# Feature-major projections: one 512-column matmul for the high weights, and the two halves summed by VectorE

## The chip, the cores and the metric

One core of a Trainium2 chip runs the whole program. The metric is the device time of one execution in microseconds (us). The engines are TensorE (PE, matmuls; PEld, its weight loads), VectorE (DVE), ScalarE (ACT), GpSimd (POOL) and SyncE (SP, which here only issues transfers).

## The reference

Four layers, each of another kind, act one after the other on x of 256 tokens by 2048 features, all in fp32. After each, `h = layer_norm(ALPHA * h + out)`.

```python
def ssd_mixer(h, w_in, ...):        # 8 groups, 64 heads of 64, state 128, chunks of 128 tokens
    z, xbc, dt = split(h @ w_in)
    xbc = silu(causal_depthwise_conv(xbc, conv_w, conv_b))       # 4 taps; 6144 features
    ... # scan over chunks, gate with silu(z), rms norm by group
    return y @ w_out
def fox_mixer(h, w_in, f_bias, w_out):   # 16 heads of 128
    q, k, v, z, f = split(h @ w_in)
    o = causal_block_attention(q, k, v, scale, cumsum(log_sigmoid(f + f_bias)))
    return (o * silu(z)) @ w_out
def mla_mixer(...):                      # 16 heads, latent q and kv, rope
    ...
    return (o * silu(z)) @ w_out
def s5_mixer(...):                       # 128 groups of 16 features, complex state of 64
    u, z = split(h @ w_in)
    ... # y = scan(u) + d * u
    y = gelu(y)
    y = y * sigmoid(y @ w_glu + b_glu) * silu(z)
    return y @ w_out
```

What matters here are the large products `h @ w` with 2048 inputs: the change touches those whose result is needed with features on the partitions.

## The kernel before

Every fp32 operand of a large product is split into a high part (rounded to the matmul's fp32r type) and a low part (the rest), and a product is the sum of three matmuls: high by high, high by low, low by high (`mm3`, L105 to L109). Weights come from memory in halves of 512 KB: SP's queue loads a half into one of seven `raw` buffers, ACT rounds it to `whi` (L100), DVE subtracts to get `wlo` (L101); there are four buffers of each. Activations hT (`hh`, `hl`) lie in SBUF with features on partitions, as 16 blocks (kb) of 128 features by 256 tokens.

A token-major projection (`proj_tok`, tile `pt`) holds activations still and moves 512 weight columns. A feature-major one (`proj_T`, L126 to L128, with its steps from L117) holds a 128x128 weight block still and moves the 256 tokens; per kb three matmuls of 256 columns add into one PSUM tile, and 16 kb make a projection. It runs 144 times with 128 weight columns: 48 in ssd (`conv`, tile `cps`), 48 in fox (q, k and z of 16 heads; `fox_q`, `fox_k`, `zps`), 16 in mla (`zps`), 16 for s5's z (`zps`) and 16 for its glu (`gps`); and twice with fewer, for ssd's dt (64, `dps`) and fox's f (16, `fps`). Readers take the result out of PSUM: `conv` by an ACT scale (L466) and three DVE multiply-adds (L468) for the taps, fox q and k by an ACT copy, the z gates by an ACT tanh and a DVE product.

Around it, in ssd: `decays` makes the running sums `acsT` (L487) from dt; POOL loads and broadcasts rows of them into `arena` (L504, L506); DVE turns these into decays (L510, L535); POOL multiplies and adds on `xs` (L557, L562, L587); after its last step in a group (the gate, L562) a normalization follows, and its result is transposed by PE into `ypt` (L605). In s5, a scan on DVE (L1165 to L1171) runs beside the z projections; then come the `near` and `far` matmuls (L1311, L1320) and transfers of `shifts` on POOL's queue (L1146).

The program is written in one order, in which `tick` (once per weight half) and `defer(n, ...)` (run n ticks later) interleave stages. A tile scheduler then orders each engine's instructions by its own cost model.

Of the kernel before, what the change touches and what calls it, by code (L numbers as in the profile page):

```python
# [11 lines left out]
F32 = mybir.dt.float32  # L12
# [18 lines left out]
class Core:  # L31
# [57 lines left out]
    def half(self, src, i, n=2048, spare=None):  # L89

        nc = self.nc
        if self.loads:
            self.loads.pop(0)()
        r = self.raw([P, n // 2], "raw")
        nc.sync.dma_start(r, src[:, i * (n // 2):(i + 1) * (n // 2)])
        if spare:
            hi, lo = (pool.tile([P, n // 2], F32R, tag=t, bufs=b, name=f"w_{t}") for pool, t, b in spare)
        else:
            hi, lo = (self.wp.tile([P, n // 2], F32R, tag=t, bufs=4, name=t) for t in ("whi", "wlo"))
        nc.scalar.copy(hi, r)  # L100
        nc.vector.tensor_tensor(lo, r, hi, op=ALU.subtract)  # L101
        return hi, lo
# [14 lines left out]
    def proj_T_steps(self, src, hT, ps, m=P, order=range(KB)):  # L117

        for i in range(2):
# [12 lines left out]
    def proj_tok(self, srcs, aT, n=512, before=None, tail=None, spare=None):  # L132
# [10 lines left out]
        while h < N:  # L143
# [26 lines left out]
    def proj_Tk(self, srcs, aT):  # L170
# [4 lines left out]
        for q, src in enumerate(srcs):  # L175
            for i in range(2):
                w = self.half(src, i)
                for j in range(2):
                    kb = 4 * q + 2 * i + j
                    a = [x[kb] for x in aT]  # L180
# [86 lines left out]
    def out_layer(self, li, parts, gb_tiles, spare, out=None):  # L267
# [10 lines left out]
        hT = ([None] * KB, [None] * KB)  # L278
# [38 lines left out]
        def turn(t, k0, nk):  # L317
            c = k0 // 4
            if t == 0 and k0 % 4 == 0:
                for i, n in enumerate("hl"):  # L320
                    x = self.hp.tile([P, 4, T], F32R, tag=f"h{n}{c}", name=f"h{n}{c}")
                    hT[i][4 * c:4 * c + 4] = [x[:, k] for k in range(4)]
                    tiles[i].append(x)
# [4 lines left out]
            hi, lo = (x[c][:, k0 % 4:k0 % 4 + nk, t * P:(t + 1) * P] for x in tiles)  # L328
# [3 lines left out]
        tiles = ([], [])  # L332
# [91 lines left out]
def ssd(C, hT, out):  # L424
# [3 lines left out]
    with C.tc.tile_pool(name="ssd", bufs=1) as sp, C.tc.tile_pool(name="ssd_c", bufs=1) as vp, C.tc.tile_pool(name="ssd_t", bufs=1) as tp:  # L428
# [45 lines left out]
        def decays():  # L474
            dps = C.acc("dps")
            C.proj_T(A["ssd_dt"], hT, dps[0:NH, 0:T], m=NH)
            x = arena[0:NH, 0:T]
            nc.vector.tensor_scalar(x, dps[0:NH, 0:T], dtb, None, op0=ALU.add)
# [137 lines left out]
        for g in range(G):  # L616
# [3 lines left out]
                           [[(C.hp, f"h{n}{c}", 1) for n in "hl"] for c in range(4)], out)  # L620


def fox(C, hT, out):
# [3 lines left out]
    with pool(name="fox", bufs=1) as fp, pool(name="fox_t", bufs=2) as tp, \  # L627
# [13 lines left out]
        fps = C.acc("fps")  # L641
        C.proj_T(A["fox_f"], hT, fps[0:H, 0:T], m=H)
        x, lf, one = V[2][0:H, 0, 0:T], V[2][0:H, 0, T:], V[2][0:H, 1, 0:T]
        nc.vector.tensor_scalar(x, fps[0:H, 0:T], fb, None, op0=ALU.add)
# [33 lines left out]
        def head(h):  # L678
# [36 lines left out]
            C.defer(1, C.attend(logits, lambda: V[h // 4], h % 4, finish, shift=cq[:, h, :]))  # L715
            zps = C.acc("zps")
            C.proj_T(A["fox_z"][h], hT, zps[:, 0:T])
            th = tp.tile([P, T], F32, tag="th", name="th")
            nc.scalar.activation(th, zps[:, 0:T], AF.Tanh, scale=0.5)
            nc.vector.scalar_tensor_tensor(th, th, 1.0, zps[:, 0:T], op0=ALU.add, op1=ALU.mult)  # L720
# [4 lines left out]
        for _ in steps:  # L725
# [3 lines left out]
                           [[(C.hp, f"h{n}{c}", 1) for n in "hl"] for c in range(4)], out)  # L729
# [20 lines left out]
def mla(C, hT, out):  # L750
# [3 lines left out]
    with C.tc.tile_pool(name="mla", bufs=1) as mp, C.tc.tile_pool(name="mla_w", bufs=1) as wp, C.tc.tile_pool(name="mla_t", bufs=2) as tp:  # L754
# [84 lines left out]
        for h in range(H):  # L839
            zps = C.acc("zps")  # L840
            C.proj_T(A["mla_z"][h], hT, zps[:, 0:T])
            th = tp.tile([P, T], F32, tag="th", name="th")
            nc.scalar.activation(th, zps[:, 0:T], AF.Tanh, scale=0.5)
            nc.vector.scalar_tensor_tensor(zs[h], th, 1.0, zps[:, 0:T], op0=ALU.add, op1=ALU.mult)
# [267 lines left out]
def s5(C, hT, out):  # L1112
# [8 lines left out]
    with C.tc.tile_pool(name="s5", bufs=1) as sp, C.tc.tile_pool(name="s5_w", bufs=1) as wp, C.tc.tile_pool(name="s5_t", bufs=1) as tp:  # L1121
# [11 lines left out]
        uX, U = {}, {}  # L1133
# [49 lines left out]
        def u_strip(ft):  # L1183
            x = uX[ft] = sp.tile([P, L, 4, NC], F32, tag=f"ux{ft}", name=f"ux{ft}")
# [42 lines left out]
        def turn2(ft, ut, w):  # L1227
            un = U[ft] = (wp if ft == 3 else sp).tile([P, 4, 4, NC], F32, tag=f"un{ft}", name=f"un{ft}")
# [54 lines left out]
        def z_tile(kb):  # L1283
            zps = C.acc("zps")
            C.proj_T(A["s5_z"][kb], hT, zps[:, 0:T])
            th = tp.tile([P, T], F32, tag="th", name="th", bufs=3)
            nc.scalar.activation(th, zps[:, 0:T], AF.Tanh, scale=0.5)
            nc.vector.scalar_tensor_tensor(zs[kb], th, 1.0, zps[:, 0:T], op0=ALU.add, op1=ALU.mult)

        yh, yl = [None] * KB, [None] * KB  # L1290
# [64 lines left out]
        def gelu(ft, yf):  # L1355
            h4 = sp.tile([P, 4, T], F32R, tag=f"ux{ft}", name=f"yh4{ft}")
            l4 = (wp if ft == 3 else sp).tile([P, 4, T], F32R, tag=f"un{ft}", name=f"yl4{ft}", bufs=1)
            for gq in range(4):
                kb = 4 * gq + ft
                yh[kb], yl[kb] = h4[:, gq], l4[:, gq]  # L1360
# [14 lines left out]
        for kb in range(KB):  # L1375
            gps = C.acc("gps")
            C.proj_T(A["s5_glu"][kb], (yh, yl), gps[:, 0:T], order=order)
            s = tp.tile([P, T], F32, tag="th", name="sg", bufs=3)
            nc.scalar.activation(s, gps[:, 0:T], AF.Tanh, bias=bg[:, kb:kb + 1], scale=0.5)
# [8 lines left out]
                           [((sp, f"ux{c}", 1), (wp if c == 3 else sp, f"un{c}", 1)) for c in range(4)], out)  # L1388
# [106 lines left out]
```

## Time and profile before

| | |
|---|---|
| median of 3 runs | 2107.67 us (2106.01 to 2112.61) |
| the profiled execution | 2112.38 us, of which the span is 2110.6 |
| granted TensorE clock in it | 0.982 |
| HBM traffic | 374.32 MB by DMA, mean 177 GB/s |
| matmul instructions | 14409 |

The profile shows one execution. PE's busy time comes from matmuls that overlap, so what one costs is read from the distance between starts; `PEclk` is the clock granted to PE, 1.00 being full speed. A row in brackets, `[7.24 <-issue]`, gives the idle time before an instruction and what ended it; `issue` means that nothing in the profile ended it. In the table of windows each pair is busy time and, in brackets, instructions.

### The profile page before, as it was taken

Reading aid. Unit: us, or ns where it says so; the run is one execution under the profiler, and the core shown is the slowest. Engines: PE = TensorE matmul, PEld = TensorE weight load, DVE = VectorE, ACT = ScalarE, POOL = GpSimd, SP = SyncE. Lnnn points to the kernel's source line nnn. Section 1 sums busy time; section 2 is a strip of 40 time slices with the busy share of each in tenths; the row PEclk is TensorE's granted clock in tenths of the full one; section 3 lists DMA queues with packets and bytes.
Section 4 is the critical chain, followed back from the end, with each engine's and each line's share of the span. In section 5 each row is a group of like instructions: output and inputs, shape, how many; then the busy total and the mean of one; then the engine's idle time right before and its main releaser. Section 6 shows DMA issues by size and latency. Waiting matters only on the chain.

```text
span 2110.6 us, 36624 instructions
## 1 busy us (share of the span) xinstructions
PE 2023.2 (96%) x14409; PEld 1834.6 (87%) x14409; DVE 1380.9 (65%) x2393; ACT 955.6 (45%) x1434; POOL 424.8 (20%) x522
## 2 busy tenths in 40 slices
PE   8999999999999999899999999999999998988997
PEld 7889888898878877799999978998888798988986
DVE  6776777677654695465555567646556787975656
ACT  5454555455443333344444444544554354444442
POOL 0211222122200027988870000000000001010002
PEclk9999999999999999899999999999999999999999
DMA  8445444544475545465666564664347555675662
GB/s 281 158 141 171 150 160 161 163 150 155 159 233 189 186 147 177 175 216 172 225 194 202 177 208 128 202 184 143 111 144 239 183 174 177 193 225 166 187 189 100
DMA packets 117292, 374.32 MB, mean 177 GB/s; under 512 B 18992, under 2 KB 23552, under 8 KB 116352
## 3 DMA queue, kind: packets, MB, share of 16 engines
q1 hardware_dynamic: 105440, 350.20, 51.9%
q0 software_dynamic: 6912, 16.14, 2.5%
q10 hardware_dynamic: 4768, 5.64, 0.8%
q8 instruction: 113, 1.85, 0.4%
q14 instruction: 59, 0.48, 0.1%
HBM read 357.81 MB, written 14.04 MB: 176 GB/s over the span
## 4 chain that ended last, share of the span: by engine, by line
PE 80%; DVE 8%; POOL 4%; DMA 4%; issue 2%; ACT 1%; SPq 0%; DVEq 0%; POOLq 0%; ACTq 0%
PE pt L109 10%; PE pt L107 10%; PE pt L108 10%; PE cps L108 4%; PE cps L107 4%; PE cps L109 4%; PE zps L107 4%; PE zps L109 4%; PE zps L108 4%; DMA shifts<-K_d 2%; DVE wlo L101 2%; PE pk L185 2%; PE pk L187 2%; PE pk L186 2%; PE gps L107 1%
## 5 line engine op out<-in xcount | busy, mean ns | idle before, releaser
L101 DVE TENSOR_TENSOR wlo<-raw,whi 128x1024 fp32r<-128x1024 f32 (+3 forms) x611 | 758.1, 1243 | 469.1 <-ACT whi L100 457.1
L100 ACT CAST whi<-raw 128x1024 fp32r<-128x1024 f32 (+3 forms) x611 | 632.0, 1036 | 803.3 <-PE pt L109 294.6
L107 PE MATMUL pt<-whi,hh 128*128 128x512 f32 (+2 forms) x716 | 281.7, 394 | 11.4 <-ACT whi L100 11.0
L109 PE MATMUL pt<-whi,hl 128*128 128x512 f32 (+2 forms) x716 | 279.8, 391 | 0.6 <-DVE hl L330 0.4
L108 PE MATMUL pt<-wlo,hh 128*128 128x512 f32 (+2 forms) x716 | 278.4, 389 | 1.6 <-DVE wlo L101 1.5
L107 PE MATMUL zps<-hh,whi 128*128 128x256 f32 x768 | 221.1, 288 | 1.0 <-ACT whi L100 1.0
L109 PE MATMUL zps<-hh,wlo 128*128 128x256 f32 x768 | 218.5, 285 | 1.3 <-DVE wlo L101 1.3
L108 PE MATMUL zps<-hl,whi 128*128 128x256 f32 x768 | 218.4, 284 | 0.0
L108 PE MATMUL cps<-hl,whi 128*128 128x256 f32 x768 | 217.6, 283 | 0.0
L109 PE MATMUL cps<-hh,wlo 128*128 128x256 f32 x768 | 217.6, 283 | 0.0
L107 PE MATMUL cps<-hh,whi 128*128 128x256 f32 x768 | 217.6, 283 | 0.0
L107 PEld LDWEIGHTS pt<-whi,hh 128*128 128x128 f32 x716 | 136.2, 190 | 39.2 <-ACT whi L100 11.4
L108 PEld LDWEIGHTS pt<-wlo,hh 128*128 128x128 f32 x716 | 136.2, 190 | 29.9 <-DVE wlo L101 3.9
L109 PEld LDWEIGHTS pt<-whi,hl 128*128 128x128 f32 x716 | 136.4, 190 | 27.4 <-issue 1.7
L107 PEld LDWEIGHTS zps<-hh,whi 128*128 128x128 f32 x768 | 148.3, 193 | 1.6 <-ACT whi L100 1.2
L109 PEld LDWEIGHTS zps<-hh,wlo 128*128 128x128 f32 x768 | 148.3, 193 | 1.5 <-DVE wlo L101 1.5
L108 PEld LDWEIGHTS zps<-hl,whi 128*128 128x128 f32 x768 | 148.3, 193 | 0.0
L108 PEld LDWEIGHTS cps<-hl,whi 128*128 128x128 f32 x768 | 147.5, 192 | 0.3
L107 PEld LDWEIGHTS cps<-hh,whi 128*128 128x128 f32 x768 | 147.4, 192 | 0.3
L109 PEld LDWEIGHTS cps<-hh,wlo 128*128 128x128 f32 x768 | 147.4, 192 | 0.1
L107 PE MATMUL pt<-whi,yh 128*128 128x512 f32 x240 | 95.8, 399 | 0.0
L108 PE MATMUL pt<-wlo,yh 128*128 128x512 f32 x240 | 95.5, 398 | 0.0
(505 smaller groups left out, 4295.5 us busy)
## 6 DMA issues: line engine op xcount, KB each, us to landing
raw<-in_ssd_z SPq DMA_DIRECT2D x64, 512.0 KB
raw<-in_ssd_x SPq DMA_DIRECT2D x64, 512.0 KB
raw<-in_ssd_o SPq DMA_DIRECT2D x64, 512.0 KB
raw<-in_fox_v SPq DMA_DIRECT2D x32, 512.0 KB
raw<-in_fox_q SPq DMA_DIRECT2D x32, 512.0 KB
raw<-in_fox_k SPq DMA_DIRECT2D x32, 512.0 KB
raw<-in_fox_z SPq DMA_DIRECT2D x32, 512.0 KB
raw<-in_fox_o SPq DMA_DIRECT2D x32, 512.0 KB
```

The lines of the kernel that those rows point to most:

```text
L100: nc.scalar.copy(hi, r)
L101: nc.vector.tensor_tensor(lo, r, hi, op=ALU.subtract)
L107: mm(ps, s[0], m[0], start=first, stop=False)
L108: mm(ps, s[0], m[1], start=False, stop=False)
L109: mm(ps, s[1], m[0], start=False, stop=last)
L185: mm(o, ws[0], a[0], start=kb == 0 and c % 2 == 0, stop=False)
L186: mm(o, ws[0], a[1], start=False, stop=False)
L187: mm(o, ws[1], a[0], start=False, stop=end)
```

## The change

The high and low halves of hT (and of s5's y) lie in one tile, and a third list gives both halves of a block as one operand of 2 pieces of 256 columns, 4 KB apart. `proj_T` then makes, per kb, one matmul of `whi` against both halves, 512 columns into both halves of a PSUM bank (tile `pT`), and one of `wlo` against the high half, 256 columns into the first. At the end DVE sums the two halves out of PSUM into an SBUF tile with one TENSOR_REDUCE (L143 after), and all readers take that tile. The 32 ACT copies of fox q and k go. Fox's attention starts one tick later. Spare buffers that held high or low parts of weights are renamed, and one tile may hold both.

```diff
     def proj_T_steps(self, src, hT, ps, m=P, order=range(KB)):
...
-                self.mm3(ps, [x[:, j * m:(j + 1) * m] for x in w], [x[order[kb]] for x in hT], kb == 0, kb == KB - 1)
+                hi, lo = (x[:, j * m:(j + 1) * m] for x in w)
+                mm(ps, hi, hT[2][order[kb]], start=kb == 0, stop=False)
+                mm(ps[:, 0], lo, hT[0][order[kb]], start=False, stop=kb == KB - 1)
...
-    def proj_T(self, src, hT, ps, m=P, order=range(KB)):
+    def proj_T(self, src, hT, out, m=P, order=range(KB)):
+        ps = self.acc("pT")[0:m].rearrange("p (n t) -> p n t", n=2)
         for _ in self.proj_T_steps(src, hT, ps, m, order):
             pass
+        self.nc.vector.tensor_reduce(out, ps.rearrange("p n t -> p t n"), AX.X, ALU.add)
...
     def new_hT(self):
-        tiles = [[self.hp.tile([P, 4, T], F32R, tag=f"h{n}{c}", name=f"h{n}{c}") for c in range(4)] for n in "hl"]
-        return tuple([x[k // 4][:, k % 4] for k in range(KB)] for x in tiles)
+        tiles = [self.hp.tile([P, 2, 4, T], F32R, tag=f"h{c}", name=f"h{c}") for c in range(4)]
+        return tuple([tiles[k // 4][:, i, k % 4] for k in range(KB)] for i in (0, 1, slice(0, 2)))
...
         def conv(src, ti, pool_tag, bufs):
-            ps = C.acc("cps")
-            C.proj_T(src, hT, ps[:, 0:T])
+            u = vp.tile([P, T], F32, tag="u", name="u", bufs=2)
+            C.proj_T(src, hT, u)
             c = vp.tile([P, T], F32, tag="conv", name="conv", bufs=2)
-            nc.scalar.activation(c, ps[:, 0:T], AF.Identity, bias=cb[:, ti:ti + 1], scale=cw[:, ti, 3:4])
+            nc.scalar.activation(c, u, AF.Identity, bias=cb[:, ti:ti + 1], scale=cw[:, ti, 3:4])
             for k in range(1, 4):
-                nc.vector.scalar_tensor_tensor(c[:, k:], ps[:, 0:T - k], cw[:, ti, 3 - k:4 - k], c[:, k:], op0=ALU.mult, op1=ALU.add)
+                nc.vector.scalar_tensor_tensor(c[:, k:], u[:, 0:T - k], cw[:, ti, 3 - k:4 - k], c[:, k:], op0=ALU.mult, op1=ALU.add)
...
             for nm in ("fox_q", "fox_k"):
-                ps = C.acc(nm)
-                C.proj_T(A[nm][h], hT, ps[:, 0:T])
                 s = tp.tile([P, T], F32, tag=nm, name=nm)
-                nc.scalar.copy(s, ps[:, 0:T])
+                C.proj_T(A[nm][h], hT, s)
...
-            C.defer(1, C.attend(logits, lambda: V[h // 4], h % 4, finish, shift=cq[:, h, :]))
+            C.defer(2, C.attend(logits, lambda: V[h // 4], h % 4, finish, shift=cq[:, h, :]))
...
         def z_tile(kb):
-            zps = C.acc("zps")
-            C.proj_T(A["s5_z"][kb], hT, zps[:, 0:T])
+            C.proj_T(A["s5_z"][kb], hT, zs[kb])
             th = tp.tile([P, T], F32, tag="th", name="th", bufs=3)
-            nc.scalar.activation(th, zps[:, 0:T], AF.Tanh, scale=0.5)
-            nc.vector.scalar_tensor_tensor(zs[kb], th, 1.0, zps[:, 0:T], op0=ALU.add, op1=ALU.mult)
+            nc.scalar.activation(th, zs[kb], AF.Tanh, scale=0.5)
+            nc.vector.scalar_tensor_tensor(zs[kb], th, 1.0, zs[kb], op0=ALU.add, op1=ALU.mult)
...
         for kb in range(KB):
-            gps = C.acc("gps")
-            C.proj_T(A["s5_glu"][kb], (yh, yl), gps[:, 0:T], order=order)
             s = tp.tile([P, T], F32, tag="th", name="sg", bufs=3)
-            nc.scalar.activation(s, gps[:, 0:T], AF.Tanh, bias=bg[:, kb:kb + 1], scale=0.5)
+            C.proj_T(A["s5_glu"][kb], (yh, yl, yb), s, order=order)
+            nc.scalar.activation(s, s, AF.Tanh, bias=bg[:, kb:kb + 1], scale=0.5)
```

ssd's dt, fox's f and z and mla's z change in the same way as the z of s5. How the instructions stand shows at three places (lines of `after` are 5 to 13 higher).

PE, in a fox head where the attention's last products (`o`) are placed between the end of q and the start of k. Before:

```order
L107 MATMUL fox_q<-hh_7220,whi 128x256
L108 MATMUL fox_q<-hl_7221,whi 128x256
L109 MATMUL fox_q<-hh_7220,wlo 128x256
L417 MATMUL o<-pt,V_7159 128x256
L418 MATMUL o<-pt,V_7159 128x128
L107 MATMUL fox_k<-hh_7064,whi 128x256
L108 MATMUL fox_k<-hl_7065,whi 128x256
L109 MATMUL fox_k<-hh_7064,wlo 128x256
```

After:

```order
L133 MATMUL pT<-h_6389,whi 128x512
L134 MATMUL pT<-h_6389,wlo 128x256
L430 MATMUL o<-pt,V_6463 128x256
L431 MATMUL o<-pt,V_6463 128x128
L133 MATMUL pT<-h_6508,whi 128x512
L134 MATMUL pT<-h_6508,wlo 128x256
```

Three rows a block became two, the first with both halves; the attention's products kept such a place.

DVE, in ssd's first group, the end of the softplus of dt (`arena`, L234 to L236), the first conv tiles (`bT`, `cT`) and the scan that makes `acsT` (L487, after L499; the order names one form of its instruction). Before:

```order
L101 TENSOR_TENSOR wlo<-raw,whi 128x1024
L235 SCALAR_TENSOR_TENSOR arena<-arena 64x256
L468 SCALAR_TENSOR_TENSOR conv<-cps,cw,conv 128x255
L236 TENSOR_SCALAR arena<-arena 64x256
L468 SCALAR_TENSOR_TENSOR conv<-cps,cw,conv 128x254
L481 SCALAR_TENSOR_TENSOR arena<-arena 64x256
L468 SCALAR_TENSOR_TENSOR conv<-cps,cw,conv 128x253
L482 TENSOR_SCALAR arena<-arena,a 64x256
L101 TENSOR_TENSOR wlo<-raw,whi 128x1024
L487 SCALAR_TENSOR_TENSOR acsT<-arena 64x128 x2
L471 SCALAR_TENSOR_TENSOR cT<-cT,conv 128x256
```

After:

```order
L106 TENSOR_TENSOR wlo<-raw,whi 128x1024
L247 SCALAR_TENSOR_TENSOR arena<-arena 64x256
L481 SCALAR_TENSOR_TENSOR conv<-u,cw,conv 128x255
L248 SCALAR_TENSOR_TENSOR arena<-arena 64x256
L481 SCALAR_TENSOR_TENSOR conv<-u,cw,conv 128x254
L249 TENSOR_SCALAR arena<-arena 64x256
L481 SCALAR_TENSOR_TENSOR conv<-u,cw,conv 128x253
L493 SCALAR_TENSOR_TENSOR arena<-arena 64x256
L143 TENSOR_REDUCE u<-pT 128x256
L494 TENSOR_SCALAR arena<-arena,a 64x256
L484 SCALAR_TENSOR_TENSOR cT<-cT,conv 128x256
L499 SCALAR_TENSOR_TENSOR acsT<-arena 64x128 x2
```

A reduce and the product for cT now stand ahead of the scan, a weight subtraction no longer does; two more reduces of 128x256 stand further ahead, and one more further behind, between L510 and L535 (after: L522 and L547).

DVE, in s5's z beside the scan. Before:

```order
L101 TENSOR_TENSOR wlo<-raw,whi 128x1024
L1288 SCALAR_TENSOR_TENSOR zs_17000<-th,zps 128x256
L1171 TENSOR_TENSOR X_17741<-X_17741,sc 128x64x16
L1165 TENSOR_TENSOR sc<-X_17741,a4s 128x1024
L101 TENSOR_TENSOR wlo<-raw,whi 128x1024
L1167 TENSOR_TENSOR sc<-X_17741,a4s 128x1024
```

After:

```order
L106 TENSOR_TENSOR wlo<-raw,whi 128x1024
L1179 TENSOR_TENSOR X_16032<-X_16032,sc 128x64x16
L143 TENSOR_REDUCE zs_15296<-pT 128x256
L1173 TENSOR_TENSOR sc<-X_16032,a4s 128x1024
L1296 SCALAR_TENSOR_TENSOR zs_15296<-th,zs_15296 128x256
L106 TENSOR_TENSOR wlo<-raw,whi 128x1024
L1175 TENSOR_TENSOR sc<-X_16032,a4s 128x1024
```

Each z projection brings one reduce to this engine; subtractions and scan keep their turns.

More of the change, by code (lines that the diff above doesn't have):

```diff
@@ L96, in half @@
         if spare:
-            hi, lo = (pool.tile([P, n // 2], F32R, tag=t, bufs=b, name=f"w_{t}") for pool, t, b in spare)
+            if len(spare) == 1:
+                (pool, t, b), = spare
+                both = pool.tile([P, 2, n // 2], F32R, tag=t, bufs=b, name=f"w_{t}")
+                hi, lo = both[:, 0], both[:, 1]
+            else:
+                hi, lo = (pool.tile([P, n // 2], F32R, tag=t, bufs=b, name=f"w_{t}") for pool, t, b in spare)
         else:
@@ L277, in out_layer @@
         gb, mean, nm, rs = [None] * 8, [None] * 2, [None] * 2, [None] * 2
-        hT = ([None] * KB, [None] * KB)
+        hT = tuple([None] * KB for _ in range(3))
         def resid(t, cb, ps):
@@ L319, in turn @@
             if t == 0 and k0 % 4 == 0:
[L320 to L323, printed above, removed]
+                x = self.hp.tile([P, 2, 4, T], F32R, tag=f"h{c}", name=f"h{c}")
+                for i, n in enumerate((0, 1, slice(0, 2))):
+                    hT[i][4 * c:4 * c + 4] = [x[:, n, k] for k in range(4)]
+                tiles.append(x)
             pt = self.aux("ptr")
@@ L327, in turn @@
             src = pt[:, 0:nk * P].rearrange("p (a b) -> p a b", a=nk)
[L328 removed]
+            hi, lo = (tiles[c][:, i, k0 % 4:k0 % 4 + nk, t * P:(t + 1) * P] for i in range(2))
             nc.scalar.copy(hi, src)
             V.tensor_tensor(lo, src, hi, op=ALU.subtract)
[L332 removed]
+        tiles = []
         def load_gb(k):
@@ L619, in ssd @@
                            [(tp, t, 1, 1) for t in ("xs0", "xs1", "xdt0", "xdt1", "xdd", "st", "rows", "gb")],
-                           [[(C.hp, f"h{n}{c}", 1) for n in "hl"] for c in range(4)], out)
+                           [[(C.hp, f"h{c}", 1)] for c in range(4)], out)
 def fox(C, hT, out):
@@ L728, in fox @@
                            [(fp, "gb0", 1, 1), (fp, "V3", 1, 1)] + [(pp, t, 1, b) for t, b in (("st", 2), ("st", 2), ("wt", 2), ("wt", 2), ("pn", 3), ("pn", 3))],
-                           [[(C.hp, f"h{n}{c}", 1) for n in "hl"] for c in range(4)], out)
+                           [[(C.hp, f"h{c}", 1)] for c in range(4)], out)
 TWO_PI = 2.0 * math.pi
@@ L1387, in s5 @@
                            [(p, t, 1, 1) for p, t in ((wp, "sc"), (sp, "XC"), (wp, "ut"), (wp, "ys"), (sp, "XA"), (sp, "a4s"), (sp, "zs0"), (sp, "zs1"))],
-                           [((sp, f"ux{c}", 1), (wp if c == 3 else sp, f"un{c}", 1)) for c in range(4)], out)
+                           [((sp, f"xu{c}", 1),) for c in range(4)], out)
 SCAN_US = 1.9
```

46 lines of the change are left out of this document (22 added, 24 removed).

## The prediction

> **What bounds the kernel now.** I read the page's busy shares first, then the timeline of TensorE (PE) for what one matmul costs from start to start, then the table of windows, stage by stage, then the waits of PE and of GpSimd (POOL).
>
> ```profile
> span 2110.6 us, 36624 instructions
> PE 2023.2 (96%) x14409; PEld 1834.6 (87%) x14409; DVE 1380.9 (65%) x2393; ACT 955.6 (45%) x1434; POOL 424.8 (20%) x522
> PE 80%; DVE 8%; POOL 4%; DMA 4%; issue 2%; ACT 1%; SPq 0%; DVEq 0%; POOLq 0%; ACTq 0%
> ```
>
> PE looks like the only bound: 96% busy, 80% of the chain that ended last. If that held everywhere, each microsecond taken from PE would come off the end. So first its price list. A matmul's own duration (the second column, 0.28 or 0.39) overlaps the next one's, so I use starts.
>
> ```profile
> 30.05 0.39 PE L108 MATMUL pt<-wlo,hh 128*128 128x512 f32 x1
> ...
> 31.87 0.28 PE L107 MATMUL dps<-hh,whi 128*64 128x256 f32 x1
> ...
> 37.31 0.28 PE L107 MATMUL cps<-hh,whi 128*128 128x256 f32 x1
> ...
> 43.07 0.28 PE L107 MATMUL cps<-hh,whi 128*128 128x256 f32 x1
> ```
>
> ```profile
> 599.74 0.40 PE L108 MATMUL pt<-wlo,yh 128*128 128x512 f32 x1
> ...
> 606.04 0.40 PE L108 MATMUL pt<-wlo,yh 128*128 128x512 f32 x1
> ```
>
> From 30.05 to 31.87 lie eight 512-column matmuls: 0.2275 us each. From 31.87 to 37.31 the 48 matmuls of 256 columns on 64 weight columns: 0.1133. From 37.31 to 43.07 the 48 of a feature-major projection (128 weight columns): 0.1200. From 599.74 to 606.04, 27 of 512 columns in an output layer: 0.2333. So one weight block (kb) of a projection costs 3 x 0.1200 = 0.360 us now.
>
> Then the stages:
>
> ```profile
> core 0: us, PE busy (x) PEld busy (x) DVE busy (x) ACT busy (x) POOL busy (x), PEclk, DMA share, GB/s
> 42.00:54.00 12.00, 12.00 (x101) 11.80 (x100) 11.90 (x26) 5.85 (x8) 0.00 (x0) 1.00 0.71 223
> 70.00:84.00 14.00, 13.49 (x80) 11.70 (x79) 13.86 (x25) 7.67 (x10) 1.19 (x3) 1.00 0.43 125
> 928.00:1094.00 166.00, 166.00 (x1453) 163.42 (x1451) 98.09 (x158) 75.30 (x133) 137.69 (x182) 1.00 0.59 199
> 1341.00:1430.00 89.00, 89.00 (x737) 88.61 (x736) 46.28 (x57) 39.99 (x56) 0.00 (x0) 1.00 0.61 182
> 1776.00:1800.00 24.00, 23.57 (x306) 22.90 (x305) 22.90 (x69) 17.70 (x35) 1.80 (x3) 1.00 0.54 167
> 1800.00:1836.00 36.00, 36.00 (x304) 35.87 (x304) 35.69 (x45) 14.40 (x19) 0.00 (x0) 1.00 0.56 169
> 1836.00:1918.00 82.00, 66.35 (x965) 64.55 (x964) 51.70 (x124) 30.26 (x51) 9.07 (x15) 0.88 0.71 209
> 1919.00:2005.00 86.00, 85.98 (x715) 85.66 (x714) 58.56 (x94) 43.60 (x66) 0.00 (x0) 1.00 0.60 184
> ```
>
> Three stages are PE's alone: the fox heads (928 to 1094), mla's z (1341 to 1430), s5's glu (1919 to 2005), with VectorE (DVE) at 52 to 68% and POOL at 83% at most. Two are DVE's as much as PE's: the first ssd group's start (11.90 of 12, 13.86 of 14) and s5's z (35.69 of 36). In 1836 to 1918 PE is not even busy. And the long ssd stage belongs to none of these:
>
> ```profile
> POOL arena L506 <- issue: 155.2, 25, 7.0
> PE ypt L605 <- ACT xs L593: 18.5, 6, 4.8
> 136.82 1.28 POOL L562 TENSOR_TENSOR xs<-xs,arena 128x512 f32<-128x512 f32 x1 [7.24 <-issue]
> 207.10 1.28 POOL L562 TENSOR_TENSOR xs<-xs,arena 128x512 f32<-128x512 f32 x1 [7.58 <-PE cps L109]
> 274.84 1.29 POOL L562 TENSOR_TENSOR xs<-xs,arena 128x512 f32<-128x512 f32 x1 [6.72 <-issue]
> ```
>
> The waits (60 to 560 us) and POOL's timeline say this: each time POOL turns from its broadcast (L506) to an elementwise product (L557, L562, L587) or back, 6 to 8 us pass in which it waits for nothing shown (155.2/25 = 6.2 before a broadcast). A group has eight such turns, some 50 to 55 of the 70.3 and 67.7 us between the gates shown. PE gets there first: in six groups it waits at ypt for what follows the gate, 18.5 us in all. The Trainium skill, GPSIMD Engine Reference, 2.1 Instruction dispatch, says that the first call to a freshly loaded kernel costs about 6 us with nothing in the profile; the trace agrees, with 6.2.
>
> **The change part by part.** *PE.* Per kb two 256-column matmuls on whi become one of 512, the third stays. The 512 row nearest to it by its operands' alignment is the 0.2275: 0.2275 + 0.1200 = 0.3475. By the two rows in exact 0.0067 steps I take 0.3467, a saving of 0.0133 per kb. Bounds: with both at their cheapest row 0.2275 + 0.1133 = 0.341 (0.019 saved), with the dear 512 row 0.2333 + 0.1200 = 0.3533 (0.0067 saved). Over all 144 x 16 = 2304 kb that is 30.7 us, but only these kb lie in stages that PE bounds:
>
> ```profile
> L107 PE MATMUL fox_k<-hh,whi 128*128 128x256 f32 x240 | 69.9, 291 | 0.0
> L107 PE MATMUL fox_q<-hh,whi 128*128 128x256 f32 x224 | 65.7, 293 | 0.0
> L107 PE MATMUL zps<-hh,whi 128*128 128x256 f32 x240 | 69.1, 288 | 0.0
> L107 PE MATMUL zps<-hh,whi 128*128 128x256 f32 x237 | 67.3, 284 | 0.0
> L107 PE MATMUL gps<-yh,whi 128*128 128x256 f32 x238 | 67.5, 284 | 0.0
> ```
>
> These are the groups by line from 892 to 1190 (fox after its first wait), 1341 to 1430 (mla) and 1919 to 2005 (glu): 240 + 224 + 240 + 237 + 238 = 1179 kb. 1179 x 0.0133 = **15.7 us off**; bounds 7.9 and 22.4. The other 1125 kb are ssd's 768, s5's z and fox's first head, where PE waits for another engine.
>
> *The reduce.* Each projection gains a DVE instruction of 512 elements from PSUM into 256.
>
> ```profile
> L101 DVE TENSOR_TENSOR wlo<-raw,whi 128x1024 fp32r<-128x1024 f32 x585 | 736.4, 1261 | 452.7 <-ACT whi L100 440.9 <-DMA raw<-in_s_u 3.9 <-DMA raw<-in_fox_z 3.3
> L330 DVE TENSOR_TENSOR hl<-ptr,hh 128x512 fp32r<-128x512 f32 x21 | 13.8, 678 | 0.2 <-ACT hh L329 0.2
> L389 DVE TENSOR_REDUCE mx<-lg 128x1 f32<-128x256 f32 x32 | 13.0, 407 | 0.0
> L388 DVE TENSOR_REDUCE mx<-lg 128x1 f32<-128x128 f32 x32 | 8.8, 274 | 0.0
> ```
>
> A reduce of 128 more elements costs 407 - 274 = 133 ns, so of 512: 407 + 2 x 133 = 0.67 us; another operation of 512 elements from PSUM measures 0.678. I take 0.68. Bounds: 0.41 (as for 256) and 1.26 (as for 1024 elements, if the stride of 256 between the two halves halves the rate). 146 of them are 99 us on an engine with 730 idle; in the PE-bound stages they are hidden by the idle third of DVE (fox: 98.09 of 166, plus some 25 x 0.68 = 17). Taken out: 32 ACT copies of fox q and k, off the path. The other readers (conv, tanh, gates) now read SBUF: the same counts and about the same price, taken as nothing, under PE or POOL.
>
> *Ssd's first group* is where DVE has no idle time. Before acsT the order now has three more 128x256 reduces and a 128x256 product for cT ahead of the scan L487, and one weight subtraction fewer (L101, 1.26): with the product at the 0.41 of L389, which has its size, 3 x 0.68 + 0.41 - 1.26 = 1.2 us. The dt reduce stands earlier, where DVE is not yet full: between nothing and 0.68, I take 0.2. POOL's first broadcasts start after the scan, the decay chain (L510, then L535) after these, and one more reduce stands inside that chain: 0.7. Sum **2.1 us later** at POOL's first elementwise product:
>
> ```profile
> 55.63 2.24 POOL L504 DMA_DIRECT2D rows<-acsT  x4 [53.70 <-DVE acsT L487]
> 84.36 2.05 POOL L557 TENSOR_TENSOR xs<-xs,dsk 128x512 f32<-128x512 f32 x2 [13.16 <-ACT xs L553]
> ```
>
> There POOL waits 13.2 us where a turn takes 6 to 8, so it waits for data, and what comes later there is later in all that follows. Bounds: 0.5 gained (reduce at 0.41, the rest hidden) and 4.2 lost (at 1.26). Groups 2 to 8 gain nothing: POOL's order is unchanged, PE's 6 x 16 x 0.0133 = 1.3 us per group become a longer wait at ypt.
>
> *S5's z.* Nine of its 16 projections stand before the first far matmuls, with the scan (L1165 to L1171) on DVE beside them. 9 x 0.68 = 6.1 us of reduces, against 1.4 us of DVE idle in the two windows: **4.7 us later**. Bounds: a gain of 1.9 (9 x 0.213, if PE bounds it) and a loss of 9.9. What follows is then later by as much, for it runs on transfers:
>
> ```profile
> PE near L1311 <- DMA shifts<-K_d: 15.7, 5, 6.8
> 1838.94 11.21 DMA shifts<-K_d
> ```
>
> These (waits from 1776 to 1925; the last chain in that stretch) are issued after the far matmuls, one after the other, so z matmuls saved between them shorten nothing. Fox's attention, put off by one more weight half, is taken as nothing: PE is busy without a break through these heads (166.00 of 166), so there is other work in its place. The merged tiles (h, xu, y4) and the spare weights change no count.
>
> *Sum.* -15.7 + 2.1 + 4.7 = -8.9. The profiled execution took 2112.38 (span 2110.6 and 1.8 around it), 4.7 over the median of the runs, 2107.67. It would become 2103.5, and the median 2098.8: I say **2099**.
>
> **A rule against the change.** The rows 0.2275 and 0.1200 say that the second half of a 512 is cheaper than a 256. The Trainium skill, TensorE: Matmul & The Clock Gate, Back-to-back issue gap, gives a warm matmul N/2.4 + 2.5 ns: by it only one 2.5 ns floor would go per kb, 0.0025 instead of 0.0133. The trace does not agree with its size (109 ns by it for 256 columns, 0.1133 and 0.1200 here), but streamed columns, the main part, are indeed unchanged.
>
> **Rivals.**
> 1. *PE bounds all* (the page's 96% taken at its word, DVE and POOL give way): -30.7, or 2077. Against it: the ypt waits and the eight turns.
> 2. *The streamed columns alone count*: if the 0.1200 is a price per moved column, the 512 form costs 2 x 0.1200 = 0.240, PE saves nothing and the reduces stay: +6.8, or 2114.5. Against it: the 0.2275. The skill's 2.5 ns per kb, named above, would take 2.9 of it back.
> 3. *The cheap end*: 0.341 per kb, -22.4 + 6.8 = -15.6, or 2092. For it: 0.1133 occurs in rows with 256 columns; against: the projection's own rows are 0.1200. *The dear end*, 0.3533: -7.9 + 6.8 = -1.1, or 2106.6, no change.
> 4. *The other side: the 512 form is two passes.* Its moving operand is two pieces 4 KB apart. If the second piece starts up anew, the matmul costs more than 0.240, the point from which PE loses. At one more step of 0.0067, 0.2467, 1179 x 0.0067 = 7.9 us come on top of 6.8: 2122, slower. Against it: PSUM and operands of 512 in one piece show no break; no row here has two pieces.
>
> **How the numbers follow.** 0.3%, 6.3 us, is about what a measurement of this kernel can tell from no change: below 2101.3 is faster, above 2114.0 slower. My forecast (0.3467 per kb, DVE terms within 3 us of mine; 2095 to 2105) has 0.47, two thirds of it below 2101.3 (0.31 and 0.16); rival 1 0.06; rival 3 0.17 at its cheap end and 0.13 at its dear one; rival 2 0.08, split at 2114; rival 4 0.04; DVE terms at their upper bounds (4.2 + 9.9: 2107.67 - 15.7 + 14.1 = 2106, over 2114 with the dear end) 0.05, of it 0.03 no change. Faster 0.31 + 0.06 + 0.17 = 0.54; same 0.16 + 0.13 + 0.04 + 0.03 = 0.36; slower 0.10. The range takes in both ends of rival 3 with 3 to 5 us of the DVE terms and leaves out rivals 1, 2 and 4: 2088 to 2112.
>
> **What would show it.** In the changed profile: starts of whi 512 and wlo 256 that alternate with a sum of 0.347 (0.360 would be rival 2, more than that rival 4, 0.341 or 0.3533 rival 3); reduces of 0.68 us; gates of POOL still 67 to 71 us apart and longer waits at ypt; the first L557 product some 2 us later; fox heads shorter by 3 x 0.213 = 0.64 us; the first far matmuls later against the start of z by 5 us. I would be wrong by a reduce above 1 us, by PE waits in fox for DVE or weights, or if POOL's turns prove to hang on PE after all.

## The result and the profile after

The changed kernel takes 2093.77 us (median of 5 runs, 2088.54 to 2099.18) against 2111.43 for the kernel before (5 runs, 2106.01 to 2114.57): ratio 0.9921, 95% interval 0.9895 to 0.9947, some 17 us faster. The forecast was 9 us. The profiled execution of after took 2099.18, that of before 2112.38: the two traces differ by 13.2 us, and these have to be found in them.

From the page of after: span, busy times, the chain that ended last.

```profile
span 2097.4 us, 31981 instructions
PE 2010.4 (96%) x12073; PEld 1707.0 (81%) x12073; DVE 1482.9 (71%) x2539; ACT 954.8 (46%) x1402; POOL 438.3 (21%) x522
PE 77%; DVE 9%; DMA 5%; POOL 4%; issue 3%; ACT 1%; SPq 0%; DVEq 0%; ACTq 0%; POOLq 0%
```

PE has 2336 matmuls fewer and is as busy as before, 96%: each of the 146 x 16 = 2336 blocks now moves its three times 256 columns with two instructions. DVE has 102 us more. What one reduce costs, from the groups by line:

```profile
L143 DVE TENSOR_REDUCE u<-pT 128x256 f32<-128x512 f32 x48 | 32.8, 684 | 3.7 <-PE pT L134 3.7
L143 DVE TENSOR_REDUCE zs<-pT 128x256 f32<-128x512 f32 x32 | 22.0, 687 | 9.8 <-PE pT L134 9.8
```

0.684 to 0.687 us; 0.68 was forecast. What a block costs, from PE's timeline: first and last start of a run without a break in mla's z, in a later fox head and in glu.

```profile
1379.63 0.39 PE L133 MATMUL pT<-h,whi 128*128 128x512 f32 x1
...
1391.42 0.39 PE L133 MATMUL pT<-h,whi 128*128 128x512 f32 x1
```

```profile
1029.82 0.40 PE L133 MATMUL pT<-h,whi 128*128 128x512 f32 x1
...
1034.76 0.40 PE L133 MATMUL pT<-h,whi 128*128 128x512 f32 x1
```

```profile
1949.68 0.40 PE L133 MATMUL pT<-y,whi 128*128 128x512 f32 x1
...
1956.39 0.40 PE L133 MATMUL pT<-y,whi 128*128 128x512 f32 x1
```

In mla 34 blocks in 11.79 us: 0.3468, as forecast. In the fox head 14 in 4.94 and in glu 19 in 6.71: 0.353, the dear end. So there are two prices; both also stand within ssd, where of the conv blocks most cost 0.353 and the last 80 (from 513.99 on) 0.347.

Where the 13.2 us lie follows from the starts of the same instruction in the two timelines:

| landmark | before | after | difference | in this stage | forecast |
|---|---|---|---|---|---|
| ssd, last residual addition (L282) | 743.25 | 735.63 | -7.6 | -7.6 | +2.1 |
| fox, last residual addition | 1281.19 | 1269.44 | -11.8 | -4.1 | -9.4 |
| mla, last residual addition | 1654.36 | 1639.71 | -14.7 | -2.9 | -3.2 |
| s5, last transpose `tp` of u (beside z's first blocks) | 1788.00 | 1778.10 | -9.9 | +4.8 | 0 |
| s5, last near matmul | 1913.87 | 1902.75 | -11.1 | -1.2 | +4.7 |
| last normalization (L313) | 2103.34 | 2089.76 | -13.6 | -2.5 | -3.2 |

The largest term has the wrong sign in the forecast, and it is in ssd. Yet the forecast's reading of ssd seems to hold: POOL's first product, three of its gates, and PE's waits over the whole program in after:

```profile
83.45 2.05 POOL L569 TENSOR_TENSOR xs<-xs,dsk 128x512 f32<-128x512 f32 x2 [13.06 <-ACT xs L565]
135.31 1.31 POOL L574 TENSOR_TENSOR xs<-xs,arena 128x512 f32<-128x512 f32 x1 [8.09 <-PE pT L134]
205.25 1.43 POOL L574 TENSOR_TENSOR xs<-xs,arena 128x512 f32<-128x512 f32 x1 [7.53 <-issue]
275.85 1.44 POOL L574 TENSOR_TENSOR xs<-xs,arena 128x512 f32<-128x512 f32 x1 [7.62 <-PE pt L114]
PE ypt L617 <- ACT xs L605: 19.5, 8, 3.8
```

The gates stand 69.9 and 70.6 us apart (70.3 and 67.7 before), with turns of 6 to 8 us as before. But the waits at ypt have not grown, as they should have, when PE was relieved. Three pairs of lines tell why: ssd's last transposes, the matmuls of the output layer up to there (group of the first of three forms, counted to 3.6 us past the start of these transposes), and the last residual addition, before and after.

```profile
586.42 0.87 PE L605 MATMUL ypt<-ident,xs 128*128 128x128 f32 x6
L107 PE MATMUL pt<-whi,yh 128*128 128x512 f32 x42 | 17.5, 416 | 0.0
743.25 0.67 DVE L282 SCALAR_TENSOR_TENSOR hres<-hres,pt 128x512 f32<-128x512 f32 x1
```

```profile
590.01 0.87 PE L617 MATMUL ypt<-ident,xs 128*128 128x128 f32 x6
L112 PE MATMUL pt<-whi,yh 128*128 128x512 f32 x58 | 23.5, 405 | 0.0
735.63 0.67 DVE L295 SCALAR_TENSOR_TENSOR hres<-hres,pt 128x512 f32<-128x512 f32 x1
```

The loop ends 3.6 us later. But 16 more of each form, 48 matmuls of 0.2333 us, have moved ahead of its end: 11.2 us of the output layer are done in PE's freed time. 3.6 - 11.2 = -7.6. In the order as built the same count stands: 160 of these matmuls ahead of the last transpose after, 112 before. I had looked at POOL's order and at DVE's, and not at what else PE had to do.

### The profile page after: what moved, and what is told of

The parts are those of the page before. It is cut to its first block, busy times and chain, and to the rows that moved or that the text cites. A ratio compares the mean times of both kernels' runs of the same rounds, so it can differ in the third digit from the quotient of the medians.

```text
span 2097.4 us, 31981 instructions
## 1 busy us (share of the span) xinstructions
PE 2010.4 (96%) x12073; PEld 1707.0 (81%) x12073; DVE 1482.9 (71%) x2539; ACT 954.8 (46%) x1402; POOL 438.3 (21%) x522
## 4 chain that ended last, share of the span: by engine, by line
PE 77%; DVE 9%; DMA 5%; POOL 4%; issue 3%; ACT 1%; SPq 0%; DVEq 0%; ACTq 0%; POOLq 0%
PE pT L133 23%; PE pT L134 12%; PE pt L113 9%; PE pt L112 9%; PE pt L114 9%; DMA shifts<-K_d 3%; DVE wlo L106 2%; PE pk L198 2%; PE pk L200 2%; PE pk L199 2%; PE yd L582 1%; PE lps L877 1%; PE lps L876 1%; DVE hres L325 1%; PE o L430 1%
## 5 line engine op out<-in xcount | busy, mean ns | idle before, releaser
L133 PE MATMUL pT<-h,whi 128*128 128x512 f32 (+2 forms) x2080 | 741.6, 400 | 0.0
L134 PE MATMUL pT<-h,wlo 128*128 128x256 f32 (+2 forms) x2080 | 585.9, 282 | 3.4 <-DVE wlo L106 3.4
L133 PEld LDWEIGHTS pT<-h,whi 128*128 128x128 f32 (+2 forms) x2080 | 389.0, 187 | 95.8 <-issue 1.2
L134 PEld LDWEIGHTS pT<-h,wlo 128*128 128x128 f32 (+2 forms) x2080 | 391.3, 188 | 6.7 <-DVE wlo L106 4.8
L112 PE MATMUL pt<-whi,h 128*128 128x512 f32 (+2 forms) x716 | 280.9, 393 | 8.6 <-ACT whi L105 8.2
L113 PE MATMUL pt<-wlo,h 128*128 128x512 f32 (+2 forms) x716 | 279.9, 391 | 2.6 <-DVE wlo L106 2.4
L114 PE MATMUL pt<-whi,h 128*128 128x512 f32 (+2 forms) x716 | 279.0, 390 | 0.3 <-DVE h L343 0.3
L112 PEld LDWEIGHTS pt<-whi,h 128*128 128x128 f32 x716 | 137.0, 192 | 35.6 <-ACT whi L105 8.7
L113 PEld LDWEIGHTS pt<-wlo,h 128*128 128x128 f32 x716 | 137.1, 191 | 31.7 <-DVE wlo L106 6.0
L114 PEld LDWEIGHTS pt<-whi,h 128*128 128x128 f32 x716 | 136.5, 191 | 26.7 <-issue 1.7
L114 PE MATMUL pt<-whi,yl 128*128 128x512 f32 x240 | 95.1, 396 | 0.0
L133 PE MATMUL pT<-y,whi 128*128 128x512 f32 x256 | 90.9, 399 | 0.0
L133 PEld LDWEIGHTS pT<-y,whi 128*128 128x128 f32 x256 | 48.1, 188 | 12.3 <-DVE y L278 0.6
```

The lines of the kernel that those rows point to most:

```text
L112: mm(ps, s[0], m[0], start=first, stop=False)
L113: mm(ps, s[0], m[1], start=False, stop=False)
L114: mm(ps, s[1], m[0], start=False, stop=last)
L133: mm(ps, hi, hT[2][order[kb]], start=kb == 0, stop=False)
L134: mm(ps[:, 0], lo, hT[0][order[kb]], start=False, stop=kb == KB - 1)
```

## The experiments

Each is compared with the kernel before run on the same chip; "changed" is the kernel after.

**e1: changed, once more.**

> The changed kernel once more, as the yardstick for the others of this series: 2094 us within 5, by both theories. Theory A (PE's work counts everywhere: where PE waits for another engine, other matmuls fill in, so each of the 2336 blocks saves, at 0.347 to 0.354 us each): PE starts of a projection in mla 0.347 apart per block, in the later fox heads and in glu 0.353. Theory B (the prediction's: ssd belongs to POOL, and only the 1179 blocks of three stages save, against 7 us lost to reduces on VectorE) says nothing else of this run.

2097.26 us (6 runs), ratio 0.9937 (0.992 to 0.9955). Its trace has ssd's last residual addition at 735.64. Blocks in mla cost 0.347 again. It gives the scatter for what follows: medians of the same kernel differ by 3.5 us (and by 6.5 in e5 and e10, which ran on two chips).

**e2: ssd's convolutions in the old form.**

```diff
-            u = vp.tile([P, T], F32, tag="u", name="u", bufs=2)
-            C.proj_T(src, hT, u)
+            u = C.proj_old(src, hT, "cps")
...
```

`proj_old` is the old form: per block three matmuls of 256 columns into PSUM, no reduce.

> The 48 conv projections of ssd in the old form (three 256-column matmuls, no reduce, readers take PSUM), all else as changed. Theory A: ssd's share is lost, 768 blocks at 0.006 to 0.013 us: 5 to 10 us slower than the changed kernel, near 2101; the output layer's matmuls that the changed order pulls ahead of ssd's last transposes (48 of them, 11 us) stand behind them again. Theory B: ssd gained nothing and lost 2 us to reduces, so this is 0 to 2 us faster than the changed kernel, near 2092.

2100.77 us, ratio 0.9954 (0.9937 to 0.9971), 3.5 slower than e1: the sign of theory A, within the scatter. The trace is clearer (the same two lines as above):

```profile
L112 PE MATMUL pt<-whi,yh 128*128 128x512 f32 x42 | 17.5, 418 | 0.0
743.15 0.68 DVE L311 SCALAR_TENSOR_TENSOR hres<-hres,pt 128x512 f32<-128x512 f32 x1
```

42 again, and ssd ends where it ended before (743.15 against 743.25). So ssd's part of the change is what brings the 7.5 us, against the forecast's loss.

**e3: ssd's convolutions without the matmul on the low weights.** The result leaves that term out; loads, splits and reduces stay.

```diff
-                mm(ps, hi, hT[2][order[kb]], start=kb == 0, stop=False)
-                mm(ps[:, 0], lo, hT[0][order[kb]], start=False, stop=kb == KB - 1)
+                mm(ps, hi, hT[2][order[kb]], start=kb == 0, stop=kb == KB - 1 and not lo_too)
+                if lo_too:
+                    mm(ps[:, 0], lo, hT[0][order[kb]], start=False, stop=kb == KB - 1)
...
```

`lo_too` is false in ssd's conv.

> As changed, but the conv projections of ssd leave out the matmul of the low weights (768 matmuls of 0.117 us, 90 us of PE's work in ssd; the weights are still loaded and split). Theory A: PE's work counts in ssd too, at least 40 of the 90 us come off: 2050 or below. Theory B: POOL's turns set the group at 67 us and more, PE only waits longer at ypt; what comes off is what can be pulled ahead from the output layer, 48 more matmuls, 11 us: near 2083.

2100.68 us, ratio 0.9959 (0.9943 to 0.9975): nothing gained with some 90 us of PE's work taken out of ssd, and neither expectation met (A 2050 or below, B 2083). The windows row (PE, PEld, DVE, ACT, POOL, then the granted clock), two gates of POOL and the end of ssd:

```profile
60.00:560.00 500.00, 427.61 (x1875) 343.68 (x1873) 395.10 (x647) 255.72 (x352) 107.77 (x99) 0.91 0.52 168
347.96 1.28 POOL L578 TENSOR_TENSOR xs<-xs,arena 128x512 f32<-128x512 f32 x1 [7.62 <-issue]
424.23 1.28 POOL L578 TENSOR_TENSOR xs<-xs,arena 128x512 f32<-128x512 f32 x1 [7.71 <-PE pT L134]
736.98 0.69 DVE L297 SCALAR_TENSOR_TENSOR hres<-hres,pt 128x512 f32<-128x512 f32 x1
```

Here PE idles (427.61 of 500) and its clock falls to 0.91 (0.98 in the same window before), and the gates are even further apart, 76.3 us in the pair shown and 72.5 on average (135.46 to 570.53, six groups). Against theory A, ssd's loop is not PE's. The order has 208 output-layer matmuls ahead of the last transposes, 96 more than before: 22.4 us; the loop ends 16.2 later (602.60 against 586.42); 16.2 - 22.4 = -6.2, and the end of ssd moved from 743.25 to 736.98, by 6.3. What PE gains in ssd is worth what the order pulls ahead, less what the loop loses, and no more. Theory B missed because the loop grew; why it did was not tried, and PE's lower clock is a possible cause that this run does not part from the rest.

**e4: the two halves next to each other.**

```diff
-                x = self.hp.tile([P, 2, 4, T], F32R, tag=f"h{c}", name=f"h{c}")
+                x = self.hp.tile([P, 4, 2, T], F32R, tag=f"h{c}", name=f"h{c}")
...
```

> As changed, but the two halves of a block lie next to each other (tile of 4 x 2 x 256 in place of 2 x 4 x 256), so that the 512 moving columns are one piece of 2 KB. If the two pieces cost something (a theory C for the 0.353 where 0.347 was expected), blocks fall to 0.347 or 0.341 in all stages: 10 to 25 us faster than the changed kernel, 2070 to 2084. Theory A and B: the pieces cost nothing, 2094 within 5, and the same two prices.

2094.14 us, ratio 0.9923 (0.9897 to 0.9949): no difference beyond the scatter, and no cheaper block: a cost of the two pieces does not show. But mla's blocks, 0.347 in after and e1, cost 0.353 here (three in 1.06 us):

```profile
1389.84 0.40 PE L133 MATMUL pT<-h,whi 128*128 128x512 f32 x1
...
1390.90 0.40 PE L133 MATMUL pT<-h,whi 128*128 128x512 f32 x1
```

**e5: POOL's elementwise work of ssd on VectorE** (the products of xdd and xs, the addition of off, the gates).

```diff
-                nc.gpsimd.tensor_tensor(xs[c], xs[c], zs[:, c], op=ALU.mult)
+                nc.vector.tensor_tensor(xs[c], xs[c], zs[:, c], op=ALU.mult)
...
```

> As changed, but the five elementwise operations that POOL does per ssd group (products of xdd and xs, the addition of off, the two gates) run on VectorE, so that POOL never turns between two kinds of work there. Theory B2 (ssd's groups are POOL's, 55 of 70 us in turns; what PE is relieved of there counts only as far as the schedule pulls output-layer matmuls ahead): the loop shortens until PE or VectorE bounds it; PE's idle and half-clock time in the loop is some 25 us, so 2075 within 8, and POOL's L518 broadcasts follow each other without 6 us of nothing. Theory A (PE's work bounds ssd too): 2094 to 2100, as VectorE only gets 40 us more to do.

2067.57 us, ratio 0.9798 (0.9783 to 0.9814): 43 us under before. POOL's timeline and a window:

```profile
275.85 3.24 POOL L518 PARTITION_BROADCAST arena<-rows  x4 [58.14 <-PE yd L582]
339.55 3.24 POOL L518 PARTITION_BROADCAST arena<-rows  x4 [58.12 <-PE yd L582]
60.00:300.00 240.00, 239.69 (x1294) 201.06 (x1293) 213.30 (x379) 132.80 (x186) 27.46 (x40) 1.00 0.50 166
```

The broadcasts of a group follow each other at once, POOL then waits 58 us for PE, a group takes 63.7 instead of some 70, and PE is busy 239.69 of 240. So POOL's work with its turns was ssd's bound. The edit takes the products off POOL too (48.2 us between 135 and 520 us in after, some 9 a group), and does not part them from the turns. The Trainium skill, GPSIMD Engine Reference, 2.1 Instruction dispatch, tells of some 6 us for a load of code at the first call to a freshly loaded kernel, with no instruction in the profile. The trace agrees with the size, and the waits go when POOL has one kind of work; that each turn is such a load is not shown.

**e6: the change in ssd, dt, f and glu only.** Fox's q, k and z, mla's z and s5's z as before.

> The changed form in ssd alone (48 conv projections, dt, and f of fox and the glu of s5 as changed; fox's q, k, z, mla's z and s5's z in the old form with the old deferral of fox's attention). Theory B2: the loop is as long as before within 4 us (POOL), 48 output-layer matmuls of 0.233 us (11 us) stand before its end instead of behind it: the output layer ends some 7 us earlier than before, 2100 with glu's 1.7 us. The prediction as it stood: ssd 2 us slower, 2110.

2102.92 us (12 runs, 2092.80 to 2113.17), ratio 0.9971 (0.9951 to 0.9992): about 6 us faster than before, where the forecast would have it at 2110. The end of ssd, at 730.97, is 12.3 us early in this trace.

```profile
730.97 0.68 DVE L311 SCALAR_TENSOR_TENSOR hres<-hres,pt 128x512 f32<-128x512 f32 x1
```

**e7: each reduce twice.**

```diff
         self.nc.vector.tensor_reduce(out, ps.rearrange("p n t -> p t n"), AX.X, ALU.add)
+        self.nc.vector.tensor_reduce(out, ps.rearrange("p n t -> p t n"), AX.X, ALU.add)
```

> As changed, but each reduce is done twice into the same tile: 146 x 0.69 = 100 us more on VectorE. The prediction's reading (VectorE is the bound at the start of ssd and in s5's z, elsewhere it has room): 4 x 0.69 + 8 x 0.69 = 8 us slower than the changed kernel, 2103. If VectorE has room there too: 2095 within 4. If it binds elsewhere as well (fox at 76%): 2110 and more.

2108.36 us, ratio 0.9987 (0.9967 to 1.0006), 11 us slower than e1, more than the 8 expected. A window at ssd's start and POOL's first product:

```profile
54.00:64.00 10.00, 9.81 (x57) 8.00 (x56) 10.00 (x21) 5.28 (x9) 2.24 (x4) 1.00 0.40 127
93.06 2.59 POOL L570 TENSOR_TENSOR xs<-xs,dsk 128x512 f32<-128x512 f32 x2 [18.45 <-ACT xs L566]
```

DVE is busy 10.00 of 10, and the product starts at 93.06 instead of 83.45: 9.6 us later (8.7 against e1's 84.34), where the first set of reduces had cost nothing (84.36 before). Of this some 2 to 3 us stand at the scan that makes `acsT` already (57.56 against 54.60 in after and 55.45 in e1); what the rest is was not taken apart. In s5's z (last tp to last near) it costs 3.7: 128.3 us against 124.6 in after.

**e8: s5's z in the old form.**

> As changed, but s5's 16 z projections in the old form, without reduces. The prediction's reading (the reduces delay the first far matmuls by 4.7 us and nothing is gained): 5 us faster than the changed kernel, 2090. Theory B2 with what the changed trace shows (the first far matmuls came earlier, as fewer z blocks stand before them): 0 to 3 us slower, 2096.

2097.79 us, ratio 0.9943 (0.9924 to 0.9961), the same as e1 and not the 2090 of the prediction's reading. In the traces the stretch from the last tp to the last near takes 126.5 us here, 125.9 before, 124.6 in after and 124.1 in e1. With e5's edit it is the other way round, 123.4 in the old form (e9) and 125.5 in the new (e10). So the sign is not settled; a loss of 4.7 stands in none of these pairs.

**e9 and e10: the kernel before with e5's edit, and e5 again.** In both 96 output-layer matmuls stand ahead of ssd's last transposes.

> The kernel before with one thing changed: the five elementwise operations per ssd group on VectorE instead of POOL. In both this and e5 96 output-layer matmuls stand ahead of ssd's last transposes, so nothing is pulled ahead by the change. Theory B2: with POOL's turns gone PE bounds ssd too, and the change then is worth every block, 2304 at 0.0067 to 0.0133 us: 15 to 31 us between this and the next run, so 2083 to 2098 here, most likely 2085. If the change's blocks in ssd save nothing even then: 2075 to 2078.

> e5 once more, as the yardstick for the two others on this chip: 2067 us within 5 by every theory.

e9 2084.04 us (2085 was expected), ratio 0.9886 (0.9865 to 0.9907); e10 2074.11, ratio 0.9832 (0.981 to 0.9853). e10 misses the expected 2067 within 5: it is e5's program on another chip, 6.5 us slower. The change is worth 0.55% here and 0.9% against e5's ratio: 10 to 19 us, around the low end of the 15 to 31 expected. The windows of e9 and e10, and the ends of ssd:

```profile
60.00:540.00 480.00, 478.93 (x3276) 437.32 (x3275) 385.72 (x667) 253.12 (x362) 41.88 (x60) 1.00 0.51 164
716.90 0.68 DVE L282 SCALAR_TENSOR_TENSOR hres<-hres,pt 128x512 f32<-128x512 f32 x1
```

```profile
60.00:540.00 480.00, 479.45 (x2594) 402.88 (x2593) 420.23 (x720) 258.81 (x366) 41.11 (x60) 1.00 0.50 168
708.52 0.68 DVE L295 SCALAR_TENSOR_TENSOR hres<-hres,pt 128x512 f32<-128x512 f32 x1
```

With PE bound in ssd and nothing pulled ahead, ssd gains 8.4 us, 0.011 per block of 768: there the blocks do count, within the bounds of 0.0067 and 0.0133. By the starts of their matmuls most of these blocks cost 0.353 in e10, which alone gives 768 x 0.0067 = 5.1 us; the other 3 were not traced.

**e11: e5 with the matmuls of two blocks regrouped.**

```diff
-                mm(ps, hi, hT[2][order[kb]], start=kb == 0, stop=False)
-                mm(ps[:, 0], lo, hT[0][order[kb]], start=False, stop=kb == KB - 1)
+                for d in range(2):
+                    mm(ps, w[0][:, (j + d) * m:(j + d + 1) * m], hT[2][order[kb + d]], start=kb + d == 0, stop=False)
+                for d in range(2):
+                    mm(ps[:, 0], w[1][:, (j + d) * m:(j + d + 1) * m], hT[0][order[kb + d]], start=False, stop=kb + d == KB - 1)
```

> e5 with the matmuls of two blocks regrouped: two of 512 on whi, then two of 256 on wlo, in place of 512, 256, 512, 256. If the two prices (0.347 and 0.353) come from the change between 512 and 256: per block 0.347 at most everywhere, or 0.341, 5 to 15 us faster than e10. If they do not: the same as e10 within 4.

2065.30 us, ratio 0.9795 (0.9773 to 0.9817), the fastest kernel here; 9 us under e10 but only 2 under e5's median. Two blocks in mla and in glu:

```profile
1329.74 0.63 PE L133 MATMUL pT<-h,whi 128*128 128x512 f32 x2
...
1332.53 0.63 PE L133 MATMUL pT<-h,whi 128*128 128x512 f32 x2
```

```profile
1899.78 0.63 PE L133 MATMUL pT<-y,whi 128*128 128x512 f32 x2
...
1901.17 0.63 PE L133 MATMUL pT<-y,whi 128*128 128x512 f32 x2
```

Eight blocks in 2.79 and four in 1.39 us: 0.348 in both places, a price between the two, where the alternating order has 0.353 in glu. Whether the 9 us are its doing or scatter these runs do not settle.

## Why the prediction was right, and where not

*The total.* Faster was right, and the time lies in the range; the size, 9 against 17 us, came from errors that partly cancel. Against the trace, ssd gave 9.7 us more than its term and s5's z 5.9 more, fox gave 5.3 less, and 4.8 were lost where the sum had nothing. That the time still lies in the range is in part luck.

*What one block and one reduce cost.* The two measured prices, 0.347 and 0.353, are the forecast's value and its dear end; the cheap end, equal columns (0.360) and the two-pass rival did not occur. The term of fox was mis-sized by this: 704 blocks at 0.0133 gave 9.4, at 0.0067 they give 4.7, and the whole stage shows 4.1 (6.3 in e1); the heads that cost 0.353 gain 48 x 0.0067 = 0.3 us each instead of 0.64 (one every 20.33 us before, every 20.06 after). The reduce was right to 1%.

*"Groups 2 to 8 gain nothing ... become a longer wait at ypt."* The first half of the reason stands: POOL sets the loop (e3, e5). The step that failed is that freed PE time must turn into waiting: 48 matmuls of the output layer went into it, 11.2 us, and e2 takes them away again with the gain. This also was ready before the result: the order of PE in the changed kernel has 160 ahead of the last transpose. The same sum holds in every trace in which POOL keeps its work: the shift of the loop's end, less 0.2333 us for each matmul pulled ahead, gives the shift of ssd's end within 0.1 us. The size is another matter. Five traces share ssd's part and the 160 (after, e1, e4, e6, e8), and their loops end from 2.9 us earlier to 4.5 later than before, so ssd ends 6.7 to 14.2 us earlier. Why the loop's length differs is open.

*"2.1 us later" at ssd's first product.* It came 0.9 us earlier in after (84.36 to 83.45), and between 0.1 earlier and 0.4 later in the four other traces with ssd's part (84.27 to 84.74): no loss. Ahead of the scan DVE has no idle time left, and the scan does come up to 0.8 us later in these four (55.71 in e8 against 54.94). But behind the scan DVE had idle time, which the forecast did not look at. From the tables of windows, one of after and then 54 to 64 us before and after:

```profile
42.00:54.00 12.00, 12.00 (x70) 10.29 (x69) 12.00 (x28) 6.35 (x9) 0.00 (x0) 1.00 0.65 210
54.00:64.00 10.00, 10.00 (x80) 9.42 (x79) 6.74 (x13) 5.25 (x10) 2.25 (x5) 1.00 0.46 142
54.00:64.00 10.00, 10.00 (x61) 8.52 (x60) 9.56 (x18) 5.47 (x10) 2.52 (x5) 1.00 0.48 159
```

DVE was busy 6.74 of these 10 us before and 9.56 after. e7, with 10.00, shows how near the limit that is: there the product comes 9.6 us later.

*"4.7 us later" in s5's z.* The first far matmuls came with fewer z blocks ahead than the nine I had counted; the group of L133 in after, from the corresponding point to the first far, has

```profile
L133 PE MATMUL pT<-h,whi 128*128 128x512 f32 x122 | 43.3, 399 | 0.0
```

122 blocks, 7.6 projections. The stretch gained 1.2 us in after, which is within what such traces differ by (e8 to e10); the loss did not come. The 4.8 us lost stand earlier, ahead of z, where nothing was forecast. Two windows around the start of s5, before and after, from the same points of the program:

```profile
1640.00:1680.00 40.00, 38.26 (x178) 30.05 (x177) 33.62 (x65) 14.97 (x19) 0.43 (x3) 1.00 0.51 182
1740.00:1776.00 36.00, 28.39 (x483) 27.38 (x483) 21.81 (x22) 11.49 (x20) 4.77 (x8) 0.95 0.66 196
```

```profile
1625.40:1668.00 42.60, 39.57 (x178) 31.34 (x177) 34.85 (x66) 15.94 (x20) 0.54 (x3) 0.96 0.53 184
1728.00:1766.20 38.20, 31.20 (x483) 29.99 (x482) 22.01 (x22) 11.47 (x20) 4.77 (x8) 0.87 0.64 190
```

The same 178 and 483 matmuls take 2.6 and 2.2 us longer, at a mean granted clock of 0.96 and 0.87 instead of 1.00 and 0.95. That slower clock is what the trace shows, and it is not the change's alone. From mla's last residual addition to the last tp it is 133.6 us before and 138.4 in after, but e5 and e10, one program on two chips, show both:

```profile
1608.40:1741.30 132.90, 124.11 (x1388) 115.46 (x1388) 99.43 (x187) 63.12 (x109) 7.45 (x15) 0.99 0.58 193
1611.90:1752.00 140.10, 128.81 (x1388) 120.34 (x1387) 99.80 (x187) 63.06 (x109) 7.42 (x15) 0.94 0.58 184
```

The longer one has the lower clock, 0.94 against 0.99, and these 7.2 us are most of what parts the two traces. The chip alone it is not: e1, on e5's chip and with the same s5 part, takes 139.2 us at 0.93. Why the clock falls in one execution and not in another stays open.

*mla and glu* came near the forecast, 2.9 and 2.5 us against 3.2 each. For mla the price fits too; glu's blocks cost 0.353, which gives only 238 x 0.0067 = 1.6 of its 2.5, so there the nearness is luck.

## What to carry to other kernels

When another engine bounds a stage, ask what else the relieved engine can do in its waiting time: in a kernel whose order is made by a scheduler the answer stands in the built order, as a count of later instructions ahead of the stage's last wait. The larger gain was the bound itself: taking POOL's elementwise work, and with it the turns, out of ssd brought 43 us together with the change, of which 25 us come without it (e9). And a reduce that is hidden now may be the last one that is: doubling it showed the room better than the busy share did.

## What the runs showed of the hardware

The same stream of 512 and 256 columns has two prices. e5 and e10 are one program, run on two chips; their first blocks of one stretch in mla's z, 17 blocks apart:

```profile
1329.78 0.39 PE L133 MATMUL pT<-h,whi 128*128 128x512 f32 x1
...
1335.67 0.39 PE L133 MATMUL pT<-h,whi 128*128 128x512 f32 x1
```

```profile
1329.33 0.40 PE L133 MATMUL pT<-h,whi 128*128 128x512 f32 x1
...
1335.32 0.40 PE L133 MATMUL pT<-h,whi 128*128 128x512 f32 x1
```

5.89 us in e5, 5.99 in e10: 0.346 and 0.352. So the program alone does not set the price. The chip alone does not either, as after shows both prices in ssd. What does stays open. The formula that the Trainium skill, TensorE: Matmul & The Clock Gate, Back-to-back issue gap, gives for an isolated warm matmul would make an estimate of 216 + 109 = 325 ns for the pair; the trace does not agree, both prices are above it by 22 to 28 ns. Taking some 90 us of matmuls out of a stage that POOL bounds made it no faster and its clock lower, 0.91 against 0.98 (e3).
